# A decoder trunk's cross-attention weights, turned by 32x32 blocks and a DRAM round trip instead of by TensorE

## The chip, the cores and the metric

The kernel runs on one core of a Trainium2 chip. Its time is the device time of one execution in microseconds (us), the median of several runs. TensorE (PE in the profile) multiplies matrices, VectorE (DVE), ScalarE (ACT) and GpSimd (POOL) work on elements, and SyncE (SP) issues most of the DMA transfers; in this kernel POOL issues the stores. Each engine takes its instructions in the order in which they stand in its own queue.

## The reference

One inference step of a decoder trunk of width 1024, for a prompt of 1024 tokens and 8 sample tokens, in float32. A normalised input goes through one wide projection; its parts feed three branches (gated linear attention, causal pooling, cross attention into 256 memory tokens), which are projected, gated, summed, projected once more and added to the input. The change lies in the third branch, for the prompt:

```
def cross_attn(q, mk, mv):
    """q: (B,T,H,Dh); mk, mv: (B,M,H,Dh)."""
    s = jnp.einsum('bthd,bmhd->bhtm', q.astype(jnp.float32), mk.astype(jnp.float32)) * (XA_HEAD_DIM ** -0.5)
    p = jax.nn.softmax(s, axis=-1)
    o = jnp.einsum('bhtm,bmhd->bthd', p, mv.astype(jnp.float32))
```

There are 4 heads of dimension 256. The sample tokens have the same attention with cached keys and values of their own.

## The kernel before

**Products and streams.** The wide projection is cut into 40 pairs of output blocks, each computed by seven products of half-size operands; a product has two slots of 12 matmuls of 128x258. Every float32 matmul is done as three (`mm3`, lines 238 to 242) on a high part and a low remainder of each operand: hi*hi, hi*lo, lo*hi. So every operand is first split: ACT writes the high part (L221, or L224 with a scale), DVE the remainder (L222 or L225). The results in PSUM banks `px` (six) are evacuated by ACT (L550 and others) and DVE (L598, L615).

**What fills the gaps.** After each slot, `fill()` moves other work on: a generator of steps, each with a cost, is advanced until its share of the work is done. In the stage from about 120 to 370 us this work is cross attention. It puts its matmuls between slots of the projection, on two PSUM banks of their own (`pz`). PE's and SP's instructions stand in the order in which the program writes them; ACT's, DVE's and POOL's are ordered by a scheduler.

**Cross attention.** The prompt is handled in 16 chunks, 4 heads with 4 chunks of 256 tokens each. `cross_steps` (L811) runs step s as a pipeline: scores of chunk s; the split of the queries of s+1 and the load of those of s+2; at s % 4 == 2 the load of the next head's memory; part of the sample tokens' work; the value matmuls of chunk s-2; more sample work; the next head's memory at s % 4 == 3; the weights of chunk s-1; three more parts of sample work. A chunk's tokens lie as j (two halves of 128) times 128 rows. `cross_scores` gives p, 128 tokens by 2 x 256 memory tokens: maxima on DVE (L688), exponentials on ACT, division on DVE (L695). The value matmuls need it the other way, memory tokens on the partitions. `cross_weights` (L698) does this by four PE transposes of 128x128 into a `pz` bank (L703), from which `split_r` writes pTh (ACT, L221) and pTl (DVE, L222) into two new tiles. `cross_values` multiplies (L714), ACT copies the result out (L715), POOL stores it as `mixsc` (L716).

**Tiles.** Tiles of 128x512 come from a ring of 14 (`R`, `NR`), reused in turn: an allocation waits until the tile of 14 allocations earlier is no longer read. A chunk takes six: xq (the queries, whose remainder is written in place), xqsh, p, pTh, pTl and xo.

**Sample tokens.** `cross_sample` is interleaved with this: the query row is stored to DRAM by POOL (`xqs`, L731), loaded again for all partitions (`qb`, L746), multiplied with cached keys on DVE (`kc`, L756); after a softmax the cached values (`vc`, four loads at a time) meet PE at L796. All loads, the projection's raw weights (`raw`, L293) too, are issued by SP in one queue.

Of the kernel before, what the change touches and what calls it, by code (L numbers as in the profile page):

```python
# [18 lines left out]
P = 128  # L19
# [5 lines left out]
NH = 4  # L25
# [8 lines left out]
CT = 256  # L34
# [13 lines left out]
def trunk_kernel(ctx: ExitStack, tc: tile.TileContext,  # L48
# [3 lines left out]
    nc = tc.nc  # L52
# [21 lines left out]
    def act(out, x, func, **kw):  # L74
        i = nc.scalar.activation(out, x, func, **kw)
        if func in (AF.Sigmoid, AF.Silu):
            table["others"].append(i)
            for e in table["exps"]:
                tc.add_manual_dep(i.ins, e.ins.name, nosync, reason="table set")
        else:  # L80
            tc.add_manual_dep(i.ins, table["load"].ins.name, nosync, reason="table set")
            table["new"].append(i)
        return i
# [15 lines left out]
    def PZ():  # L99
        return ps.tile([P, 512], F32, tag="pz", name="pz", bufs=2)  # L100

    def shaped(t, shape):
        n = math.prod(shape)
        t = t[:, :n]
        if len(shape) == 2:
            t = t.rearrange("p (a b) -> p a b", a=shape[0])
        elif len(shape) == 3:
            t = t.rearrange("p (a b c) -> p a b c", a=shape[0], b=shape[1])
        return t
# [4 lines left out]
    def R(shape, dt=F32, name="r"):  # L114

        return shaped(wk.tile([P, 512], dt, tag="ring", name=name, bufs=NR), shape)
# [16 lines left out]
    def tiny(w, name="t", bufs=8):  # L133
        return wk.tile([P, 16], F32, tag="t", name=name, bufs=bufs)[:, :w]


    ident = cp.tile([P, P], F32, name="ident")
# [63 lines left out]
    def scratch(n, name, shape):  # L201
        return [dr.tile(list(shape), F32, name=f"{name}{i}") for i in range(n)]

    PAIR = (P, 4, HT)
    xq_scr, v_scr = scratch(NH, "xqs", (NS, 256)), scratch(NH, "vs", (NS, 256))
    acc_scr = [scratch(NK, f"acc{n}_", (P, TT)) for n in range(2)]
    mkv_scr = [scratch(NH, f"mkvs{o}", (P, 2, DV)) for o in range(2)]
    al_scr = scratch(2, "als", (P, HT))
# [9 lines left out]
    def split(dst_hi, dst_lo, src, scale=None):  # L218

        if scale is None:  # L220
            last["hi"] = nc.scalar.activation(dst_hi, src, AF.Copy)  # L221
            last["lo"] = nc.vector.tensor_tensor(dst_lo, src, dst_hi.bitcast(F32), op=ALU.subtract)  # L222
        else:
            nc.scalar.activation(dst_hi, src, AF.Copy, scale=scale)  # L224
            nc.vector.scalar_tensor_tensor(dst_lo, src, scale, dst_hi.bitcast(F32), op0=ALU.mult, op1=ALU.subtract)  # L225

    def split_r(src, shape, name, scale=None):
        hi, lo = R(shape, F32R, name + "h"), R(shape, F32R, name + "l")
        split(hi, lo, src, scale)
        return hi, lo  # L230

    def split_in(x, shape, name, scale=None):

        hi, lo = R(shape, F32R, name + "h"), x.bitcast(F32R)
        split(hi, lo, x, scale)
        return hi, lo

    def mm3(out, lh, ll, rh, rl, start, stop, more=False):

        nc.tensor.matmul(out, lhsT=lh, rhs=rh, start=start, stop=False, skip_group_check=more)  # L240
        nc.tensor.matmul(out, lhsT=lh, rhs=rl, start=False, stop=False, skip_group_check=more)  # L241
        nc.tensor.matmul(out, lhsT=ll, rhs=rh, start=False, stop=stop, skip_group_check=more)  # L242
# [401 lines left out]
    def mix_chunk(n, h, c):  # L644
        return mix_scr[n][h][:, :, c * CT:(c + 1) * CT]

    def loaded(src, shape, name, alloc=None):
        t = (alloc or R)(shape, name=name)
        nc.sync.dma_start(out=t, in_=src)
        return t  # L650
# [8 lines left out]
    cross = {}  # L659

    def cross_load(h):
        cross["raw", h] = [loaded(mkv_scr[o][h], [2, DV], "mkv") for o in range(2)]

    def cross_memory(h):
        mk, mv = cross["raw", h]
        t = PZ()
        for i in range(2):
            for a in range(2):
                nc.tensor.transpose(t[:, i * NM + a * P:i * NM + (a + 1) * P], mk[:, a, i * P:(i + 1) * P], ident)
        cross["mk", h] = split_r(t.rearrange("p (i m) -> p i m", i=2), [2, NM], "mkT")  # L670
        cross["mv", h] = split_in(mv, [2, DV], "mvs")
# [7 lines left out]
    def cross_scores(h, c):  # L679
        xh, xl = cross["q", h, c]  # L680
        mh, ml = cross["mk", h]
        t = PZ()
        for j in range(2):
            for i in range(2):
                cs = slice(j * P, (j + 1) * P)
                mm3(t[:, j * NM:(j + 1) * NM], xh[:, i, cs], xl[:, i, cs], mh[:, i], ml[:, i], i == 0, i == 1)
        nm = tiny(2, "nm")
        nc.vector.tensor_reduce(nm, t.rearrange("p (j m) -> p j m", j=2), axis=AX.X, op=ALU.max, negate=True)  # L688
        p = R([2, NM], name="p")
        sm = tiny(2, "sm")  # L690
        for j in range(2):
            act(p[:, j], t[:, j * NM:(j + 1) * NM], AF.Exp, bias=nm[:, j:j + 1], accum_out=sm[:, j:j + 1])
        nc.vector.reciprocal(sm, sm)
        for j in range(2):
            nc.vector.tensor_scalar(p[:, j], p[:, j], sm[:, j:j + 1], None, op0=ALU.mult)  # L695
        cross["p", h, c] = p

    def cross_weights(h, c):  # L698
        p = cross["p", h, c]
        t = PZ()  # L700
        for a in range(2):
            for j in range(2):
                nc.tensor.transpose(t[:, (2 * a + j) * P:(2 * a + j + 1) * P], p[:, j, a * P:(a + 1) * P], ident)  # L703
        cross["pT", h, c] = split_r(t.rearrange("p (a t) -> p a t", a=2), [2, CT], "pT")

    def cross_values(h, c):
        ph, pl_ = cross["pT", h, c]
        vh, vl = cross["mv", h]
        g = R([2, CT], name="xo")
        t = PZ()  # L710
        for i in range(2):
            cs = slice(i * P, (i + 1) * P)
            for a in range(2):
                mm3(t[:, i * CT:(i + 1) * CT], vh[:, a, cs], vl[:, a, cs], ph[:, a], pl_[:, a], a == 0, a == 1)  # L714
        nc.scalar.activation(g, t.rearrange("p (i t) -> p i t", i=2), AF.Copy)  # L715
        nc.gpsimd.dma_start(out=mix_chunk(2, h, c), in_=g)  # L716

# [93 lines left out]
    def cross_steps():  # L811
        def scores(n):
            cross_scores(n // 4, n % 4)

        def memory(n):
            if n % 4 == 0:
                cross_memory(n // 4)

        def weights(n):
            cross_weights(n // 4, n % 4)  # L820

        def values(n):
            cross_values(n // 4, n % 4)

        samples = chain_of(cross_sample(h) for h in range(NH))
        cross_load(0)
        cross_memory(0)
        cross_fetch(0, 0)
        yield 2
        cross_queries(0, 0)  # L830
        cross_fetch(0, 1)
        for s in range(16 + 2):
            if s < 16:
                scores(s)
                yield 3
                if s + 1 < 16:
                    cross_queries(*divmod(s + 1, 4))
                if s + 2 < 16:
                    cross_fetch(*divmod(s + 2, 4))
            if s % 4 == 2 and s < 14:  # L840
                cross_load(s // 4 + 1)
            if s >= 1:
                yield next(samples, 0)
            if 0 <= s - 2:
                values(s - 2)
                yield 1.7
            if s >= 1:
                yield next(samples, 0)
            if s % 4 == 3 and s < 15:
                memory(s + 1)  # L850
                yield 2
            if 0 <= s - 1 < 16:
                weights(s - 1)
                yield 1.7
            for _ in range(3):
                if s >= 1:
                    yield next(samples, 0)
        yield from samples

    def chain_of(gens):  # L860
        for g in gens:
            yield from g
# [423 lines left out]
    with tc.issue_after(last["hi"].ins), tc.issue_after(last["lo"].ins):  # L1286
        prepare(1)
        for j in (4, 6):
            r = squares(x_t[j:j + 2], 4 + j)
# [104 lines left out]
    for u, (o, n, d) in enumerate(units):  # L1394
# [11 lines left out]
        for t, (c0, cw) in zip(ts, CH):  # L1406
            cs = slice(c0, c0 + cw)
# [48 lines left out]
    for hf, order in enumerate(ORDERS):  # L1456
        for tb in order:
# [13 lines left out]
            if hf == 0:  # L1471
                x = (E([D], name="y") if tb < 8 else RAW("ys").rearrange("p a b -> p (a b)"))[:m]
                nc.sync.dma_start(out=x, in_=x_p[tb * P:(tb + 1) * P] if tb < 8 else x_s)
                rows_[tb], sums[tb] = x, wk.tile([P, 4], F32, tag="yq", name="yq", bufs=9)[:m]
            x, sq = rows_[tb], sums[tb]
# [5 lines left out]
            n, a = hf, 0  # L1481
            for b in ends:
                t = ts if tb == 8 else begun.pop(0) if begun else PX()
                cs = slice(512 * hf + a, 512 * hf + b)
# [12 lines left out]
                n, a = n + 1, b  # L1497
# [3 lines left out]
            if end:  # L1501
                r = rstd_of(sq[:, 2:3], 1.0 / D, more=so_far)
# [6 lines left out]
            r = rstd_of(sq[:, 0:1], 1.0 / D, m)  # L1509
# [34 lines left out]
```

## Time and profile before

| What | Number |
|---|---|
| Median of 3 runs | 1454.77 us (1454.15 to 1455.24) |
| Span of the profiled execution | 1455.4 us, 0.6 above the median |
| PE busy | 1430.4 us, 98% |
| DVE, ACT, POOL busy | 62%, 47%, 11% |
| DMA | 259.46 MB, mean 178 GB/s |

The profile is of one execution, and its span is that execution's own time. A row of a group gives the line, the engine, the operation, out<-in with the tiles' names, the shape and the count, then the busy time, the mean ns of one, and the idle time of the engine just before, with what ended it ("<-PE pz L703"). In a timeline a row is start, duration, engine, line. PEld is PE's weight load, which runs beside its matmuls; a matmul's duration is longer than the distance to the next, since matmuls overlap in the pipeline. SPq is SP's DMA queue. A landing is the time from the issue of a DMA until its data is there.

### The profile page before, as it was taken

The page shows a single profiled execution, that of the slowest core. Times are in us where ns is not written, and L with a number is a line of the kernel's source. Part 1 is how long each engine was busy: PE and PEld are TensorE (multiplying, and loading weights), DVE is VectorE, ACT ScalarE, POOL GpSimd, SP SyncE. Part 2 cuts the span into 40 slices and gives each one's busy share as a digit, 9 for nine tenths or more (in the row PEclk, how much of TensorE's full clock was granted, in tenths as well). Part 3 has the DMA queues.
Part 4 walks back from the last instruction along what each step waited for, and adds up shares of the span by engine and source line. Part 5 has one row for each costly group of instructions (what it writes and reads, how often), then busy time and mean ns, then how long its engine had stood idle before and what let it go on. Part 6 is the DMA issues. An engine that isn't in the chain of part 4 may idle for free.

```text
span 1455.4 us, 28240 instructions
## 1 busy us (share of the span) xinstructions
PE 1430.4 (98%) x10817; PEld 1369.2 (94%) x10817; DVE 896.6 (62%) x2075; ACT 688.4 (47%) x1591; POOL 159.0 (11%) x297
## 2 busy tenths in 40 slices
PE   7999999999999999999999999999999999999998
PEld 6899999999899999999999999999999999999876
DVE  6955756656576767766756668785672443544436
ACT  5744444444565666656554445454472333233312
POOL 3211111111011111111111111110010000000000
PEclk9999999999999999999999999999999999999999
DMA  9345675756445453553544455464595677632633
GB/s 322 127 165 183 204 226 173 227 174 201 158 146 178 149 176 121 166 175 118 180 139 141 153 187 187 147 197 155 191 304 159 219 252 249 231 120 67 230 119 116
DMA packets 181843, 259.46 MB, mean 178 GB/s; under 512 B 20540, under 2 KB 130900, under 8 KB 181700
## 3 DMA queue, kind: packets, MB, share of 16 engines
q1 hardware_dynamic: 159900, 183.87, 40.8%
q0 software_dynamic: 21664, 73.59, 13.3%
q8 instruction: 85, 1.39, 0.4%
q14 instruction: 50, 0.41, 0.1%
q10 hardware_dynamic: 144, 0.20, 0.0%
HBM read 180.47 MB, written 77.59 MB: 177 GB/s over the span
## 4 chain that ended last, share of the span: by engine, by line
PE 87%; DMA 6%; DVE 4%; ACT 1%; issue 1%; SPq 0%; DVEq 0%; POOL 0%; ACTq 0%
PE px L240 25%; PE px L241 24%; PE px L242 24%; PE pz L242 2%; PE pz L240 2%; PE pz L241 2%; DMA qb<-xqs 2%; DMA raw<-in_w_in_dram 1%; DMA vc<-in_cache_mem_v_dram 1%; DVE kc L756 1%; PE pz L942 1%; PE pz L924 1%; DMA wm<-in_w_mv_dram 1%; PE pz L796 1%; PE pz L926 1%
## 5 line engine op out<-in xcount | busy, mean ns | idle before, releaser
L242 PE MATMUL px<-bh,wbl 128*128 128x384 f32 (+1 forms) x576 | 184.1, 320 | 0.0
L241 PE MATMUL px<-bl,wbh 128*128 128x384 f32 (+1 forms) x576 | 184.1, 320 | 0.0
L240 PE MATMUL px<-bh,wbh 128*128 128x384 f32 (+1 forms) x576 | 183.8, 319 | 0.0
L550 ACT ACTIVATE r<-px 128x258 f32<-128x258 f32 x240 | 89.8, 376 | 46.7 <-PE px L242 46.1
L240 PEld LDWEIGHTS px<-bh,wbh 128*128 128x128 f32 x576 | 108.4, 188 | 0.0
L241 PEld LDWEIGHTS px<-bl,wbh 128*128 128x128 f32 x576 | 108.2, 188 | 0.0
L242 PEld LDWEIGHTS px<-bh,wbl 128*128 128x128 f32 x576 | 108.2, 188 | 0.0
L240 PE MATMUL px<-ot,s1h 128*128 128x258 f32 x320 | 93.9, 293 | 0.0
L240 PE MATMUL px<-ot,s3h 128*128 128x258 f32 x320 | 93.4, 292 | 0.0
L240 PE MATMUL px<-o,a12h 128*128 128x258 f32 x320 | 93.3, 291 | 0.0
L240 PE MATMUL px<-o,s4h 128*128 128x258 f32 x320 | 93.0, 291 | 0.2 <-DVE c L615 0.2
L240 PE MATMUL px<-o,a11h 128*128 128x258 f32 x320 | 92.9, 290 | 0.0
L240 PE MATMUL px<-ot,a22h 128*128 128x258 f32 x320 | 92.9, 290 | 0.0
L240 PE MATMUL px<-ot,s2h 128*128 128x258 f32 x320 | 92.3, 288 | 0.0
L241 PE MATMUL px<-o,a11h 128*128 128x258 f32 x320 | 91.0, 284 | 0.3 <-DVE o L222 0.3
L242 PE MATMUL px<-o,a12l 128*128 128x258 f32 x320 | 90.7, 283 | 0.0
L241 PE MATMUL px<-o,a12h 128*128 128x258 f32 x320 | 90.6, 283 | 0.0
L241 PE MATMUL px<-ot,s2h 128*128 128x258 f32 x320 | 90.1, 282 | 0.5 <-DVE ot L222 0.5
L242 PE MATMUL px<-o,a11l 128*128 128x258 f32 x320 | 90.6, 283 | 0.0
L241 PE MATMUL px<-ot,a22h 128*128 128x258 f32 x320 | 90.5, 283 | 0.0
L242 PE MATMUL px<-ot,s3l 128*128 128x258 f32 x320 | 90.4, 283 | 0.0
L241 PE MATMUL px<-ot,s3h 128*128 128x258 f32 x320 | 90.4, 282 | 0.0
(469 smaller groups left out, 4587.3 us busy)
## 6 DMA issues: line engine op xcount, KB each, us to landing
raw<-in_w_in_dram SPq DMA_DIRECT2D x80, 512.0 KB, 3.8
msc<-c POOLq DMA_DIRECT2D x24, 516.0 KB, 4.4
brsc<-c POOLq DMA_DIRECT2D x24, 516.0 KB, 4.0
sig<-msc SPq DMA_DIRECT2D x24, 516.0 KB, 6.0
mix<-mixsc SPq DMA_DIRECT2D x48, 256.0 KB, 4.5
brr<-brsc SPq DMA_DIRECT2D x48, 256.0 KB, 5.3
wbr<-in_w_branch_dram SPq DMA_DIRECT2D x24, 512.0 KB, 5.5
acc<-sig POOLq DMA_DIRECT2D x16, 516.0 KB, 6.1
```

The source lines that it names most:

```text
L240: nc.tensor.matmul(out, lhsT=lh, rhs=rh, start=start, stop=False, skip_group_check=more)
L241: nc.tensor.matmul(out, lhsT=lh, rhs=rl, start=False, stop=False, skip_group_check=more)
L242: nc.tensor.matmul(out, lhsT=ll, rhs=rh, start=False, stop=stop, skip_group_check=more)
L550: nc.scalar.activation(r, acc[c][:, :QT], AF.Copy)
L756: nc.vector.tensor_tensor_reduce(kc[:, a, :], kc[:, a, :], qb[:, bb, :], scale=1.0, scalar=0.0, op0=ALU.mult, op1=ALU.add, accum_out=sc[:, ...
L796: nc.tensor.matmul(t[32 * j:32 * j + 32, :DV], lhsT=pm[:, a, 4 * i + j, :], rhs=vc[j][:, a, :], start=a == 0, stop=a == 1)
L924: nc.tensor.matmul(t[0:64, 0:P], lhsT=ki[:, 0:64], rhs=qi, start=True, stop=True)
L926: nc.tensor.transpose(t[:, P:2 * P], kt, ident)
L942: nc.tensor.matmul(to, lhsT=kiqi[:, 1, cs], rhs=st, start=False, stop=True)
```

## The change

The PE transposes go. At the end of `cross_scores` DVE transposes p in blocks of 32x32 in one instruction (into pt), and POOL stores the result with four DMAs into a DRAM scratch `pts`, so that the blocks come to their places there, in 256 runs of 256 B each DMA. A new `cross_turned(h, c)` lets SP load the turned weights back as tile pT, 128 x 2 x 256, in runs of 1 KB. It is called in step s for chunk s-1, behind the query load of s+2 and ahead of the sample work. `cross_weights` then only splits pT: the high part into a new tile, the remainder in place. The tokens of a chunk come back in another order (q, j, c: four blocks, two halves, 32 tokens); `cross_values` reads them so that its result is in the old order, with the moving operand in runs of 32 values. A chunk takes seven ring tiles: xq, xqsh, p, pt, pT, pTh, xo.

```diff
+    pt_scr = scratch(4 * NH, "pts", (8, 32, 4, 64))
...
             nc.vector.tensor_scalar(p[:, j], p[:, j], sm[:, j:j + 1], None, op0=ALU.mult)
-        cross["p", h, c] = p
+        pt = R([512], name="pt")
+        nc.vector.transpose(pt.rearrange("p (b j c) -> p j b c", j=2, c=32), p.rearrange("p j (b c) -> p j b c", c=32))
+        for q in range(4):
+            nc.gpsimd.dma_start(out=pt_scr[4 * h + c][:, :, q, :].rearrange("b r x -> r b x"),
+                                in_=pt[32 * q:32 * q + 32].rearrange("r (b x) -> r b x", b=8))
 
     def cross_weights(h, c):
-        p = cross["p", h, c]
-        t = PZ()
-        for a in range(2):
-            for j in range(2):
-                nc.tensor.transpose(t[:, (2 * a + j) * P:(2 * a + j + 1) * P], p[:, j, a * P:(a + 1) * P], ident)
-        cross["pT", h, c] = split_r(t.rearrange("p (a t) -> p a t", a=2), [2, CT], "pT")
+        cross["pT", h, c] = split_in(cross["pr", h, c], [2, CT], "pT")
+
+    def cross_turned(h, c):
+        cross["pr", h, c] = loaded(pt_scr[4 * h + c].rearrange("(a b) r q x -> (b r) a (q x)", a=2), [2, CT], "pT")
 
     def cross_values(h, c):
...
-                mm3(t[:, i * CT:(i + 1) * CT], vh[:, a, cs], vl[:, a, cs], ph[:, a], pl_[:, a], a == 0, a == 1)
+                rh, rl = (x[:, a].rearrange("p (q j c) -> p j q c", q=4, j=2) for x in (ph, pl_))
+                mm3(t[:, i * CT:(i + 1) * CT].rearrange("p (j q c) -> p j q c", j=2, q=4), vh[:, a, cs], vl[:, a, cs],
+                    rh, rl, a == 0, a == 1)
...
             if s % 4 == 2 and s < 14:
                 cross_load(s // 4 + 1)
+            if 0 <= s - 1 < 16:
+                cross_turned(*divmod(s - 1, 4))
             if s >= 1:
                 yield next(samples, 0)
```

On POOL the four stores of each chunk stand ahead of the store of an earlier chunk's result; the eight of the first two chunks stand ahead of the store of the sample's query row (`xqs`). On DVE the block transpose stands, at most chunks, right between the division that completes p and the remainder split of the next chunk's queries.

SP's queue at the loads of the first cached values, before:

```order
L649 DMA xq<-xqsc_171 128x2x256
L293 DMA raw<-in_w_in_dram 128x4x256
L649 DMA xq<-xqsc_171 128x2x256
L649 DMA vc<-in_cache_mem_v_dram 128x2x256 x4
L293 DMA raw<-in_w_in_dram 128x4x256
```

And after:

```order
L650 DMA xq<-xqsc_187 128x2x256
L650 DMA pT<-pts_134 128x2x256
L294 DMA raw<-in_w_in_dram 128x4x256
L650 DMA xq<-xqsc_187 128x2x256
L650 DMA pT<-pts_135 128x2x256
L650 DMA vc<-in_cache_mem_v_dram 128x2x256 x4
L294 DMA raw<-in_w_in_dram 128x4x256
```

The reload of chunk s-1 stands behind the query load of chunk s+2, ahead of the raw weights and the cached values.

ACT's queue around the first chunk's high split, before (a, s are weights of the projection, r copies out of px, qn the sample's query row):

```order
L730 ACTIVATE qn<-pz 8x256
L221 ACTIVATE pTh<-pz 128x512
L221 ACTIVATE a22h<-raw 128x512
L550 ACTIVATE r_1705<-px 128x258
L75 ACTIVATE p,sm<-pz,nm 128x256 x2
```

And after:

```order
L735 ACTIVATE qn<-pz 8x256
L222 ACTIVATE a22h<-raw 128x512
L551 ACTIVATE r_1729<-px 128x258
L222 ACTIVATE pTh<-pT 128x512
L222 ACTIVATE a12h<-raw 128x512
L75 ACTIVATE p,sm<-pz,nm 128x256 x2
```

The high split has moved behind the weight split a22h and one copy, and stands ahead of the weight split a12h and the exponentials of chunk 2.

## The prediction

> **What bounds the kernel now.** I read the page first: busy time and the chain that ended last.
>
> ```profile
> PE 1430.4 (98%) x10817; PEld 1369.2 (94%) x10817; DVE 896.6 (62%) x2075; ACT 688.4 (47%) x1591; POOL 159.0 (11%) x297
> PE 87%; DMA 6%; DVE 4%; ACT 1%; issue 1%; SPq 0%; DVEq 0%; POOL 0%; ACTq 0%
> ```
>
> TensorE (PE) is busy for 98% of the span and carries 87% of the chain. Next came the table of windows, since a share of the span is an average over stages. Its columns are the window, its length, then busy us and instructions of PE, PE's weight loads, VectorE (DVE), ScalarE (ACT) and GpSimd (POOL), the granted clock, the DMA engines' share and GB/s.
>
> ```profile
> 120.00:370.00 250.00, 243.49 (x2053) 236.02 (x2052) 155.07 (x403) 110.95 (x267) 28.22 (x53) 0.99 0.61 192
> 370.00:700.00 330.00, 328.02 (x2694) 312.67 (x2693) 228.00 (x601) 203.45 (x554) 41.89 (x70) 1.00 0.47 154
> 700.00:1100.00 400.00, 398.81 (x3292) 395.12 (x3291) 274.83 (x605) 203.89 (x450) 47.69 (x78) 1.00 0.56 182
> ```
>
> The first row is the cross-attention stage, where all of the change lies. PE is idle there for 6.5 of 250 us, and in the two stages behind for 2.0 of 330 and 1.2 of 400: what the stage gives back, the rest carries to the end almost whole. DVE is busy 62% of the stage, ACT 44%, POOL 11%. Third, the list of PE's waits between 120 and 375 us (total, times, longest):
>
> ```profile
> PE pz L796 <- DMA vc<-in_cache_mem_v_dram: 1.9, 2, 1.5
> PE pz L782 <- DVE ps L777: 1.5, 1, 1.5
> PE pz L240 <- ACT xqsh L224: 1.4, 1, 1.4
> PE pz L242 <- DVE xq L225: 1.3, 2, 1.0
> PE pz L240 <- DVE pTl L222: 1.2, 1, 1.2
> PE pz L770 <- DVE mkTl L222: 0.7, 1, 0.7
> ```
>
> Eight waits, 8.0 us, none of them of the transposes for their input and none of a projection for a weight. So in this stage PE's own issue time is the limit, and an instruction taken from PE is worth what it took of that.
>
> **What is removed.** One chunk's four transposes in PE's timeline (start, duration), the same tile in the group over all 16 chunks, and a second chunk:
>
> ```profile
> 182.28 0.28 PE L242 MATMUL px<-ot,a22l 128*128 128x258 f32 x1
> 182.40 0.60 PE L703 MATMUL pz<-ident,p 128*128 128x128 f32 x4
> 182.96 0.28 PE L241 MATMUL px<-o,a12h 128*128 128x258 f32 x1
> L703 PE MATMUL pz<-ident,p x64: 270/272/275, 137.3 to 357.5; 128*128 128x128 f32 x64
> 198.20 0.28 PE L242 MATMUL px<-ot,s3l 128*128 128x258 f32 x1
> 198.88 0.28 PE L241 MATMUL px<-ot,s3h 128*128 128x258 f32 x1
> ```
>
> The matmul ahead of the group starts at 182.28, the second one behind it at 182.96. Without the group two ordinary steps lie between; such a step is 0.12 us (182.28 to 182.40). The group costs 0.68 - 0.24 = 0.44 us, and the second chunk the same (198.20 to 198.88). Times 16 that is **7.0 us**. The four lines' own busy time, 0.60 x 16 = 9.6 us, counts overlap with the pipeline and is the upper bound.
>
> Also removed is one use of the two PSUM banks (pz) per chunk. At one place PE waited 1.2 us because the low split, pTl, still read such a bank (the last row but one of the waits): now the split reads SBUF, and the wait can go. That is **1.2 us**, or 0 if the bank is held by something else.
>
> **What is added on ACT and DVE.** The splits stay, one hi and one lo per chunk, with another source. Groups of the stage, last numbers busy us and mean ns:
>
> ```profile
> L688 DVE TENSOR_REDUCE nm<-pz 128x2 f32<-128x512 f32 x16 | 11.0, 688 | 9.8 <-PE pz L242 9.8
> L222 DVE TENSOR_TENSOR pTl<-pz,pTh 128x512 fp32r<-128x512 f32 x16 | 11.0, 687 | 5.7 <-ACT pTh L221 5.1 <-DMA mixsc<-xo 0.5
> L225 DVE SCALAR_TENSOR_TENSOR xq<-xq,xqsh 128x512 fp32r<-128x512 f32 x16 | 11.0, 685 | 0.0
> L224 ACT ACTIVATE xqsh<-xq 128x512 fp32r<-128x512 f32 x16 | 10.1, 631 | 0.0
> L221 ACT ACTIVATE pTh<-pz 128x512 fp32r<-128x512 f32 x16 | 9.5, 595 | 5.9 <-PE pz L703 5.4 <-DMA mixsc<-xo 0.2
> L240 PE MATMUL pz<-pTh,mvsh 128*128 128x256 f32 x64 | 18.1, 283 | 0.0
> ```
>
> From SBUF the hi split takes 631 instead of 595 ns, 0.6 us in all, and the lo split 685 instead of 687: nothing on an ACT that is idle over half of the stage. The new 32x32 transpose is not in the trace. All DVE rows over 128x512 elements lie at 0.69 us, whatever they do; I take that, 16 x 0.69 = 11 us, which lifts DVE from 155 to 166 of 250. Were it twice as slow, DVE would be at 71%. It stands ahead of the next chunk's query split in DVE's order, and the scores wait for that split at one place near the start of the stage:
>
> ```profile
> 131.52 0.39 PE L242 MATMUL pz<-mkTh,xq 128*128 128x256 f32 x1 [0.98 <-DVE xq L225]
> ```
>
> There 0.98 becomes 0.98 + 0.69: **+0.7 us**. The only other wait for xq, 0.3 us of the 1.3 listed, is of the first scores, ahead of any p.
>
> **The round trip.** Rows for its parts: a POOL issue, the landings (KB each, median us), the last from the start of the program, whose 64 KB go in short runs.
>
> ```profile
> 148.93 0.69 POOL L716 DMA_DIRECT2D mixsc<-xo  x1 [1.87 <-ACT xo L715]
> mixsc<-xo POOLq DMA_DIRECT2D x15, 256.0 KB, 3.9
> xq<-xqsc SPq DMA_DIRECT2D x14, 256.0 KB, 5.1
> xqs<-qn POOLq DMA_DIRECT2D x4, 8.0 KB, 1.6
> wa<-in_w_in_dram POOLq DMA_DIRECT2D x1, 64.0 KB, 7.4
> ```
>
> Each chunk issues 4 stores of 64 KB on POOL, 256 runs each like mixsc<-xo: 4 x 0.69 = 2.8 us, 44 us in the stage on an engine busy 28 of 250. Such a store lands in 1.6 to 7.4 us; I take 3.9, the row of equally many runs. The reload has the size and the runs of xq: 5.1 us behind an issue of 0.53. From p to pT that makes 0.69 + 2.8 + 3.9 + 0.5 + 5.1 = **13.0 us**, 10.7 to 16.5 by the bounds. What there is of time, at the first chunk and at a late one whose reload stands behind xq in SP's queue:
>
> ```profile
> 129.92 0.61 DVE L695 TENSOR_SCALAR p<-p,sm 128x256 f32<-128x256 f32 x2
> 140.84 0.39 ACT L550 ACTIVATE r<-px 128x258 f32<-128x258 f32 x1 [0.93 <-PE px L242]
> 146.41 0.28 PE L240 MATMUL pz<-pTh,mvsh 128*128 128x256 f32 x1
> 283.83 0.53 SPq L649 DMA_DIRECT2D xq<-xqsc  x1
> 289.95 0.60 ACT L221 ACTIVATE pTh<-pz 128x512 fp32r<-128x512 f32 x1 [1.03 <-PE pz L703]
> 300.24 0.28 PE L240 MATMUL pz<-pTh,mvsh 128*128 128x256 f32 x1
> ```
>
> First chunk: p is done at 130.5, pT lands at 143.5. In the new order ACT comes to the hi split behind the r copy, at 141.2, and would stand for 2.3 us, with a weight split and the exponentials of the next chunk but one queued behind it; DVE's lo split likewise, with a row maximum behind. The value matmuls want pT at 146.4, and hi and lo splits of 1.3 us end at 144.8: late for ACT, in time for PE. Late chunk: xq is issued at 283.83, the reload right behind at 284.4, pT is there at 289.5 to 290.0, and ACT split pT at 289.95 in any case. From 300.24 on PE needs it, 10 us later. So the trip is hidden but for short stands of ACT and DVE, which PE sees only if a PSUM evacuation behind them is late.
>
> What is queued behind the reload on SP: key, value, query and weight loads of the stage. Where p's trip is not over, they wait too. At the first chunk SP stood for the sample's query row anyway (issued at 137.25 by POOL, now behind eight stores). The next tight place is this:
>
> ```profile
> 175.62 2.31 SPq L649 DMA_DIRECT2D vc<-in_cache_mem_v_dram  x4
> 184.39 0.42 PE L796 MATMUL pz<-vc,pm 128*32 128x256 f32 x4
> vc<-in_cache_mem_v_dram SPq DMA_DIRECT2D x32, 256.0 KB, 4.1
> ```
>
> Four loads issued by 177.9 are used at 184.39; with a landing of 4.1 us some 2.4 us are spare. The reload, now ahead of them, takes 0.5 of it, and more if its ring tile is free late. I set the new waits of this kind, and those of ACT and DVE, at **1.5 us** in all, between 0 and 4 (two late places at 2 us each).
>
> **The memory system.** All packets of the stage's two large queues:
>
> ```profile
> q1 hardware_dynamic: 33008, 34.80, 47.0%
> q0 software_dynamic: 3776, 12.95, 13.3%
> ```
>
> 47.0% of 16 engines over 250 us is 1880 us, 57 ns for a packet of 1.05 KB. The reloads are 4096 of those: 233 us, 5.8% of the engines. The stores are 16,384 runs of 256 B, between 14 ns (by bytes) and 57 ns: 5.7% to 23%. The DMA share goes from 0.61 to 0.72 to 0.90. The Trainium skill, page "DMA: Bandwidth & Descriptors", section "Specifications", says that transfers below 512 B make the DMA engine read, modify and write. By it the upper end is the likelier, and the time is that of the late trip below. No row here has runs of 256 B by themselves. I keep the loads' times as they are and leave the upper end to a rival.
>
> **Sum.** -7.0 - 1.2 + 0.7 + 1.5 = -6.0 us on the profiled span of 1455.4, or 1449.4. The median of the runs is 1454.77, 0.6 below that span, so the time told is **1448.8**. About 0.2%, 2.9 us, is what a measurement here tells from no change (the three runs differ by 1.1).
>
> **Rivals.**
>
> *Strided weights on PE (slower).* The 192 value matmuls (three groups of 64 as the row of pTh,mvsh) now read their moving operand in runs of 32 values, 128 B, in permuted order. No matmul of the trace reads so. If such a matmul no longer streams at one step, it goes from 0.12 towards its own 0.283 us: at most +31 us, at half rate +23. From +31 ns each it eats the 6.0; I take half rate, -6.0 + 23.0 = **1471.8**. For it: the order is new to PE. Against: within each run nothing changes. The Trainium skill, "Advanced Engine Details and Errata", section "Memory Cachelines", says SBUF works in 16-byte lines, and two hits on a line hide the latency; it calls non-contiguous access slow for matmuls only under PSUM. The PSUM output stays in order here, so by that page the cost would be none. Chance 0.06.
>
> *The trip is late at every chunk (slower).* With the DMA engines at 0.9, or POOL's issues slower beside a busier DVE, the 13.0 us and the splits' 1.3 pass the 15.9 that the first chunk has from p (130.5) to the values (146.4). Then ACT and DVE stand at every chunk with evacuations behind them, and loads stand behind the reload on SP. It eats the gain when PE loses 0.37 us per chunk (6.0 / 16). At twice that, 0.75 us, it is 1448.8 + 12 = **1460.8**. For it: a DMA share of 0.61 already, and the first chunk's reserve of 1.6 us (144.8 to 146.4), which the upper bound of 16.5 us passes. Against: 10 us of reserve at the late chunk. Chance 0.08. A milder form, at a few chunks alone, eats 3 to 6 us: **1453.3** with 4.5, no difference to be told. Chance 0.16.
>
> *Nothing is gained,* because the pipeline hides the transposes and PE takes the same time without them: 1454.8. Against it the 0.44 us, twice to the hundredth. Chance 0.02.
>
> *More is gained:* the 9.6 of the transposes, the 1.2, and no new wait: 1454.77 - 10.8 = **1444.0**. For it: banks pz come free earlier at every chunk. Chance 0.08.
>
> **Numbers.** The forecast has 0.60. With the larger gain, faster has 0.68; the milder late trip and nothing gained make 0.18 for no change; late trips at every chunk and strided weights make 0.14 for slower. The range goes from 1445, just above the larger gain, to 1458, which holds the 4 us bound of the new waits and the milder late trip. It leaves out the strided weights (0.06), most of the late trips (0.07) and half of the larger gain (0.04).
>
> **What would show it.** Right: no PE rows of the transposes, value matmuls still 0.12 us apart, PE's idle time in the stage within 3 us of 6.5, end of stage some 6 us earlier. Wrong: value matmuls further apart, or PE waits on ACT's or DVE's weight splits, on px evacuations, or on vc and raw loads of more than 3 us in sum.

## The result, and the profile after

The changed kernel takes 1463.15 us (four runs, 1460.83 to 1465.33), the kernel before 1454.46 us beside it. The ratio is 1.0057, 95% interval 1.0044 to 1.0071: **slower by 0.57%, 8.3 us**, where 6.0 us less was forecast, and outside the range given. The profiled execution was a mild one, 2.3 below the median, with a span of 1459.1 us, only 3.7 above the profile of before. (A span is in nearly all runs 1.7 us shorter than the time told; by that the profile of before is of an execution of some 1457 us, above its median.) The runs without a profile cannot be taken apart, so what follows explains 3.7 us row by row and the rest by the comparisons of times.

The page after, busy time and the chain that ended last:

```profile
PE 1427.9 (98%) x10753; PEld 1362.6 (93%) x10753; DVE 905.2 (62%) x2091; ACT 687.0 (47%) x1591; POOL 196.1 (13%) x361
PE 89%; DMA 4%; DVE 4%; issue 1%; ACT 1%; SPq 1%; POOL 0%; DVEq 0%; ACTq 0%
```

The 64 transposes are gone (10817 to 10753 matmuls), and PE is still 98% busy. The windows show where it was lost:

```profile
120.00:370.00 250.00, 235.32 (x1924) 223.79 (x1923) 161.68 (x415) 107.16 (x263) 65.55 (x117) 0.99 0.71 223
370.00:700.00 330.00, 329.86 (x2717) 314.44 (x2716) 226.80 (x597) 201.76 (x548) 41.34 (x69) 1.00 0.48 154
```

In the cross-attention stage PE is now idle for 14.7 us, against 6.5; the next stage has no loss. PE's waits between 120 and 380 us:

```profile
PE pz L801 <- DMA vc<-in_cache_mem_v_dram: 5.4, 3, 4.5
PE pz L775 <- DVE sc L761: 4.0, 3, 2.3
PE pz L241 <- ACT xqsh L225: 2.6, 2, 1.4
PE pz L243 <- DVE xq L226: 1.0, 2, 0.8
PE pz L787 <- DVE ps L782: 1.0, 1, 1.0
PE pz L241 <- ACT p L75: 0.6, 1, 0.6
```

Together 14.6 us, against 8.0. Of these, 10.4 us are waits not for anything of the prompt's 16 chunks, but for the **sample tokens' own attention**: the cached values (vc), the scores that DVE sums up (sc) and the weights of the softmax (ps). Before, these three had 3.4 (vc 1.9, ps 1.5, sc none). All other waits are 4.2 us, against 4.6. The waits for turned weights, which the change concerns, are not in the list at all.

The same two projection matmuls in both timelines, at the stage's two ends, before:

```profile
119.65 0.28 PE L241 MATMUL px<-ot,a22h 128*128 128x258 f32 x1
381.12 0.28 PE L241 MATMUL px<-o,s4h 128*128 128x258 f32 x1
```

and after:

```profile
118.21 0.28 PE L242 MATMUL px<-ot,a22h 128*128 128x258 f32 x1
384.81 0.28 PE L242 MATMUL px<-o,s4h 128*128 128x258 f32 x1
```

The stage took 261.5 us and takes 266.6: +5.1 with 7.0 us of transposes taken out, so some 12 us came in. 6.6 are the waits, net. The rest hides in what counts as busy. The sample tokens' value products (128 matmuls in both), before and after:

```profile
L796 PE MATMUL pz<-vc,pm 128*32 128x256 f32 x128 | 9.9, 386 | 1.9 <-DMA vc<-in_cache_mem_v_dram 1.9
```

```profile
L801 PE MATMUL pz<-vc,pm 128*32 128x256 f32 x128 | 14.4, 413 | 5.5 <-DMA vc<-in_cache_mem_v_dram 5.4
```

4.5 us more busy time with the same work. It comes in eight rows of 16: the first, second, third and fifth took 1.07, 1.22, 1.07 and 1.07 us before and take 2.08, 1.88, 3.83 and 3.18, with slow clock or a late part of the values inside them; only the last two are shorter than before. The worst place, SP's queue, before:

```profile
235.66 0.53 SPq L649 DMA_DIRECT2D xq<-xqsc  x1
236.89 11.13 SPq L649 DMA_DIRECT2D vc<-in_cache_mem_v_dram  x8
```

SP's queue after, with the DVE and PE rows that belong to it:

```profile
237.81 0.53 SPq L650 DMA_DIRECT2D xq<-xqsc  x1
242.59 0.37 SPq L650 DMA_DIRECT2D pT<-pts  x1
243.52 12.43 SPq L650 DMA_DIRECT2D vc<-in_cache_mem_v_dram  x7
...
241.81 0.71 DVE L698 STREAM_TRANSPOSE pt<-p 128x512 f32<-128x512 f32 x1
...
251.27 3.83 PE L801 MATMUL pz<-vc,pm 128*32 128x256 f32 x16 [4.48 <-DMA vc<-in_cache_mem_v_dram]
```

The reload of one chunk is not issued behind xq at 238.3, but at 242.6, in the moment in which DVE's block transpose ends (241.81 + 0.71). With stores of the chunk long landed, it waits for its **ring tile**. This is the eighth reload, and the transpose is the ninth: it belongs to the next chunk, whose p is taken only four allocations ahead of the reload's tile. So the tiles are not handed out strictly in turn, as "Tiles" above has it: what the wait fits is that the reload got the tile which that p had just left. The values' loads behind it are issued 6.6 us later than before (2.2 of it because xq itself is later), and PE stands for them for 4.48 us. Over the stage SP's list of waits has two rows that the trip brings:

```profile
SPq L650 <- DMA pts<-pt: 12.3, 4, 7.4
SPq L650 <- DVE pt L698: 9.8, 3, 4.1
```

The first is the trip itself, not yet over (7.8 us at the first reload) or holding a tile that a load of xq needs (4.5 us); the second is three reloads that wait for the next chunk's transpose. Back at that place, PE is then slow as well, as the granted clock (third number from the end) shows in two windows behind the wait:

```profile
252.00:255.40 3.40, 3.40 (x15) 1.29 (x15) 0.00 (x0) 0.27 (x1) 0.00 (x0) 0.50 0.09 30
256.00:259.40 3.40, 3.40 (x31) 3.40 (x30) 1.38 (x2) 0.91 (x2) 0.00 (x0) 1.00 0.84 272
```

Half the clock for 3.4 us: a long wait costs 1.7 us on top of itself. (The 15 matmuls against 31 show more than the clock, since most of them are the late value products.) The stage has two such stretches, both behind a wait of the sample chain (the other from 170 us on, behind a wait for sc). Before, it had one, at 124.5 us, behind a wait of the prompt's first scores for xqsh.

### The profile page after: what moved, and what is told of

It is laid out like the page before. It is cut to its first block, busy times and chain, and to the rows that moved or that the text cites. A ratio compares the mean times of both kernels' runs of the same rounds, so it can differ in the third digit from the quotient of the medians.

```text
span 1459.1 us, 28334 instructions
## 1 busy us (share of the span) xinstructions
PE 1427.9 (98%) x10753; PEld 1362.6 (93%) x10753; DVE 905.2 (62%) x2091; ACT 687.0 (47%) x1591; POOL 196.1 (13%) x361
## 4 chain that ended last, share of the span: by engine, by line
PE 89%; DMA 4%; DVE 4%; issue 1%; ACT 1%; SPq 1%; POOL 0%; DVEq 0%; ACTq 0%
PE px L241 25%; PE px L242 25%; PE px L243 25%; PE pz L243 2%; PE pz L242 2%; PE pz L241 2%; DMA qb<-xqs 2%; DMA vc<-in_cache_mem_v_dram 2%; PE pz L949 1%; PE pz L801 1%; PE pz L931 1%; DMA x<-in_x_prompt_dram 1%; DVE kc L761 1%; PE pz L933 1%; PE pz L893 0%
## 5 line engine op out<-in xcount | busy, mean ns | idle before, releaser
L241 PE MATMUL px<-ot,s3h 128*128 128x258 f32 x320 | 93.3, 291 | 0.0
L243 PE MATMUL px<-ot,s1l 128*128 128x258 f32 x320 | 90.4, 283 | 0.0
```

## The experiments

Five theories, as they were set up and fell. **A**: the reload stands in SP's one queue, and the sample tokens' loads behind it come late. **B**: a chunk takes seven ring tiles instead of six, so loads wait for a tile. **C**: the trip's packets slow other transfers. **D**: DVE's added transposes make the work behind them late. **E**, formed after the first eight runs: the sample tokens' chain stands in PE's fixed order without any reserve, so whatever touches it is paid, by A to D alike. (In the profile of before PE already waits for vc and ps, 3.4 us, so at these reads there is none.) Every kernel was timed beside the kernel before, and a ratio to it is given with its interval; "0.31%" below is of some 1454 to 1455 us. One caution holds for all: ACT's, DVE's and POOL's orders are made anew for each kernel, so an effect of 0.2 to 0.3% may partly be that order. In this section PE's waits are those between 120 and 380 us.

**The trip left out.** The stores, the reload and the DVE transpose are gone, and unturned weights go to the value matmuls:

```
-        pt = R([512], name="pt")
-        nc.vector.transpose(...)
...
+        cross["pr", h, c] = p
```

> The changed kernel without the trip: no transpose on DVE, no stores, no reload; p itself is split and goes to the value matmuls unturned (so the attention's result is another), still read in strided runs, six ring tiles a chunk. All theories: the saving alone, 16 x 0.44 = 7.0 us and perhaps 1.2 of the bank wait, 1446 to 1449 us, stores and waits for vc and sc as before. If the strided reading by the value matmuls cost something, it would be seen here: at half rate 1470.

1451.02 us, 0.9979 (0.9968 to 0.9989): 3.1 us gained, not 6 to 8. So even with no trip at all less than half of the saving arrives. In its profile the stage has nearly the same PE idle time as before, but three stretches at half clock instead of one; before, and without the trip:

```profile
120.00:380.00 260.00, 252.01 (x2124) 243.27 (x2123) 157.61 (x411) 114.43 (x276) 29.81 (x56) 0.99 0.62 195
```

```profile
120.00:380.00 260.00, 251.62 (x2094) 242.20 (x2093) 162.45 (x426) 115.74 (x285) 30.21 (x57) 0.98 0.62 195
304.20:307.60 3.40, 3.40 (x22) 2.98 (x15) 0.37 (x1) 0.39 (x1) 0.00 (x0) 0.50 0.51 160
```

The last row is one of the two extra stretches. Both stand behind reads of the sample tokens: a wait of 3.1 us ahead of the value products (L797), for which the profile names no releaser, and one of 2.3 us for ps. So with nothing added, PE waits 5.7 us at the sample tokens' reads, against 3.4: part of what is taken from PE comes back as waits, as it would if PE only arrived earlier at reads whose data come no sooner.

**The reload on POOL's queue.**

```
-        cross["pr", h, c] = loaded(pt_scr[...]..., [2, CT], "pT")
+        cross["pr", h, c] = R([2, CT], name="pT")
+        nc.gpsimd.dma_start(out=cross["pr", h, c], in_=pt_scr[...]...)
```

> The changed kernel with one edit: the reload of the turned weights is issued by POOL, behind that chunk's four stores, and no longer by SP. Theory A (the reload stands in SP's one queue, and the sample tokens' key, query and value loads behind it come late): PE's waits for sc and vc fall from 9.4 us to about the 2 of before, no clock drop beyond the one of before, 1447 to 1451 us. Theory B (seven ring tiles a chunk instead of six: loads wait for a free tile): the same tiles are taken, so SP still waits for them, 1457 to 1463. Theory C (the trip's packets slow all landings): as many packets, 1458 to 1463.

1460.82 us, 1.0045 (1.0030 to 1.0059), against 1.0057 of the change. Theory A alone is not it: the intervals overlap. PE's waits for vc and sc did fall, from 9.4 to 3.0 us, nearly as A had it, but one for ps rose to 5.1, and all waits together are 15.3 us, against 14.6.

**Transpose and stores added to the kernel before.**

```
         cross["p", h, c] = p
+        pt = R([512], name="pt")
+        nc.vector.transpose(...)
+        for q in range(4):
+            nc.gpsimd.dma_start(out=pt_scr[...], in_=pt[32 * q:32 * q + 32]...)
```

> The kernel before, its PE transposes kept, with the block transpose on DVE and the four stores per chunk added and their result unused; no reload. Seven ring tiles a chunk. Theory A: nothing stands in SP's queue, so only the 0.7 us of the first query split: 1454 to 1457. Theory B: loads wait for tiles as in the changed kernel, 1459 to 1465. Theory C: two thirds of the trip's added DMA time are the stores', landings of vc and qb grow from 4.0 and 4.1 towards 4.8 and 5.3: 1459 to 1465.

1473.73 us, 1.0138 (1.0122 to 1.0154). 19 us, with no reload at all, so a loss of this size needs no A. It isn't quite the change's loss, though: besides 5.6 us for vc, PE here waits 5.8 us for pTl, the split of the PE transposes' result, which the changed kernel doesn't have.

**A larger ring.**

```
-NE = 30
-NR = 14
+NE = 29
+NR = 16
```

> The changed kernel with a ring of 16 tiles instead of 14, the room taken from one of the 30 tiles of the projection's operands. Theory A: SP's reload still waits for the stores, little changes, 1457 to 1463. Theory B: SP no longer waits for tiles (its waits for DVE pt, 9.8 us, and for PE pz, 21 us, shrink by half or more) and the loss goes: 1447 to 1452. Theory C: 1458 to 1463.

1509.98 us, 1.0390 (1.0367 to 1.0413). A miss: the missing operand tile costs by itself, all along the program (between 700 and 1100 us, where no cross attention is left, PE is idle for 10.3 us, against 1.2), and nothing about the ring follows.

**A seventh ring tile and nothing else,** in the kernel before:

```
+        nc.vector.memset(R([512], name="pt")[:, :8], 0.0)
```

> The kernel before with nothing but a seventh ring tile per chunk: it is taken where the changed kernel takes pt, and DVE writes 8 columns of it, used by nobody. No transpose, no stores, no reload. Theory B (ring: loads at the head of SP's queue wait for a tile that matmuls of the same step still read, and the cached keys and values behind them come late): most of the loss of the added stores' kernel, 1462 to 1475 us, with SP's waits for PE pz up from 20.6 us. Theory C (packets) and theory D (the DVE transpose): no change, 1453 to 1456.

1458.99 us, 1.0031 (1.0017 to 1.0044). The time agrees with theory B, at a smaller size than expected. The list of SP's waits has a row that the kernel before has not, with the dummy's own name:

```profile
SPq L649 <- DVE pt L697: 18.4, 5, 9.8
```

PE does not wait longer in this profile, 7.8 us against 8.0, which is of one of the kernel's fastest executions (1456.5 us). So how the tile costs the time is not shown, and part of 0.31% may be the order.

**Transpose and stores with pt in a tile of its own,** in the kernel before:

```
-        pt = R([512], name="pt")
+        pt = w2
```

> The kernel before with the block transpose and the four stores per chunk added and unused, as in the added stores' kernel, but pt in a tile of its own (the place of the gate weights w2, which are then loaded at the end of the stage), so six ring tiles a chunk. Theory B: 1454 to 1458, against 1473.7 with pt in the ring. Theories C and D: still 1468 to 1475.

1462.92 us, 1.0051 (1.0036 to 1.0066). Against the same work with pt in the ring, 1.0138, the tile is worth over 12 us here, more than the dummy. In the ring it is held until its stores have landed; that this makes the difference is not shown, since in the ring version's profile only 0.6 us of waits are listed as for these stores. And 0.51%, 7.4 us, remain without it.

**The changed kernel with pt in a tile of its own** (the same edit):

> The changed kernel with pt in a tile of its own (the place of w2, loaded at the end of the stage): six ring tiles a chunk as before the change, the trip itself unchanged. Theory B: the loss goes, 1447 to 1452 us, PE's waits in the stage 8 us or less. Theory A (the reload stands in SP's queue): little changes, 1457 to 1462, since SP still waits for the stores. Theory C: 1457 to 1462.

1457.36 us, 1.0018 (1.0007 to 1.0029). About two thirds of the loss against the kernel before are gone, but it isn't faster. At the place shown above SP now issues as the kernel before did:

```profile
235.52 0.47 SPq L648 DMA_DIRECT2D pT<-pts  x1
...
236.82 12.94 SPq L648 DMA_DIRECT2D vc<-in_cache_mem_v_dram  x8
```

The reload follows xq at once, and the values' loads stand at 236.82, before at 236.89. At this place B is shown: the tile delayed the queue. But PE's waits did not fall to 8 us or less, as B had it: they are 14.0 us, against 14.6 with pt in the ring, of them 8.0 for vc, ps and sc. They stand at other reads now.

**The same with the reload on POOL.**

> The same with the reload issued by POOL as well, so that nothing of the trip stands in SP's queue and six ring tiles are taken. Theory B alone: as with SP's reload, 1447 to 1452. Theories A and B both at work: better than that kernel by 2 us or more, 1446 to 1449. Theory C: 1457 to 1462 still.

1463.55 us, 1.0059 (1.0044 to 1.0073): worse than with SP's reload. Why was not settled; the two differ in POOL's, DVE's and ACT's orders too. PE waits 10.9 us for ps, sc and vc. So in every version of the changed kernel up to here that computes the whole, the sample tokens' reads cost PE 8 to 11 us of waits, at changing places.

**Without the sample tokens' attention:** its loads, products, softmax and stores are left out of the kernel before, and of the changed kernel, with the spacing of the steps kept:

```
-        samples = chain_of(cross_sample(h) for h in range(NH))
+        costs = [0.5] * 2 + [1.2, 1] * 3 + [1] + [0.5] + [1.2, 0.5] * 2 + [1.2, 0.5, 0.5] * 2 + [1.2]
+        samples = iter([1.2, 0.5, 0.5] + costs * NH)
```

> The kernel before without the sample tokens' cross attention: none of its loads, DVE, ACT, PE or POOL work, its result left at zero; the order and the spacing of all else as they were. It serves as the base for the changed kernel treated alike. Theory E (the sample tokens' chain of query row, products on DVE, softmax, cached values stands in PE's fixed order without reserve, and what the trip adds makes it late): PE's waits in the stage go to 3 us or less, 1438 to 1446 us by the matmuls left out and the waits. Theory C (packets slow the loads of the weights and queries): the same here, since this is the base.

> The changed kernel, seven ring tiles and SP's reload, without the sample tokens' cross attention, as the kernel before was cut. Theory E: what the trip delays is gone, so the saving shows whole: 6 to 8 us below the kernel before cut in the same way. Theories B and C (tiles or packets make the prompt's own loads late): at or above that kernel, -1 to +8 us.

1432.13 us (0.9858, 0.9843 to 0.9873) and 1426.17 us (0.9816, 0.9803 to 0.9829), four runs each. **Here the change gains 6.0 us**, with seven ring tiles, SP's reload and the trip's packets all in place. The same two matmuls at the stage's ends, the kernel before without samples:

```profile
125.11 0.38 PE L240 MATMUL px<-o,a12h 128*128 128x258 f32 x1
380.07 0.28 PE L241 MATMUL px<-o,s4h 128*128 128x258 f32 x1
```

and the changed kernel without them:

```profile
124.16 0.28 PE L241 MATMUL px<-o,a12h 128*128 128x258 f32 x1
371.90 0.28 PE L242 MATMUL px<-o,s4h 128*128 128x258 f32 x1
```

254.96 against 247.74 us: 7.2 less. PE's waits within these bounds are 0.9 us in the one,

```profile
PE pz L242 <- DVE xq L225: 0.9, 1, 0.9
```

and 2.0 in the other:

```profile
PE pz L241 <- ACT xqsh L225: 1.2, 1, 1.2
PE pz L243 <- DVE xq L226: 0.8, 1, 0.8
```

The first has one stretch at half clock, at its start, and the second none:

```profile
125.10:128.50 3.40, 3.40 (x18) 3.40 (x17) 1.24 (x4) 1.54 (x5) 0.00 (x0) 0.50 0.33 131
```

7.2 is thus 1.7 of clock, less 1.1 of waits, and 6.6 for the transposes. (The first profile is of the slowest of its four runs, 1436.1 us.) This is the run that decides: the saving is there, and the prompt's own path hides the trip. What eats it is the sample tokens' chain, at whose reads PE stands in the traces above. That these reads are late because they have no reserve in PE's order is argued: without the chain the stage's load is smaller as well, with the DMA engines busy 52% between 120 and 380 us instead of 71%. The load does not make the prompt's own reads late: at all other reads PE waits 4.2 us in the changed kernel, 4.6 in the one before.

**The parts alone, in the kernel before.** The transpose alone, into its own tile:

```
+        pt = w2
+        nc.vector.transpose(pt..., p...)
```

> The kernel before with only the block transpose on DVE added, 16 x 0.7 us, into a tile of its own and unused; no stores, six ring tiles. Of the 7.8 us that transpose and stores cost together with pt in its own tile: theory D (DVE, in order, comes later to the sample chain and the query splits) puts most here, 1459 to 1463; theory C almost none, 1455 to 1457.

1458.12 us, 1.0033 (1.0023 to 1.0044). The stores alone, of p in its ring tile:

```
+        pt = p.rearrange("p j m -> p (j m)")
+        for q in range(4):
+            nc.gpsimd.dma_start(out=pt_scr[...], in_=pt[32 * q:32 * q + 32]...)
```

> The kernel before with only the four stores per chunk added, of p itself as it stands and unused; no block transpose, six ring tiles (p's is held until it is stored). Theory C (256-byte runs slow the other transfers): most of the 7.8 us, 1460 to 1464. Theory D: almost nothing, 1455 to 1457.

1467.24 us, 1.0095 (1.0079 to 1.0110). That is more than transpose and stores cost together from an own tile (1.0051), so most of it would be p's tile, held until the stores have landed; the profile has only 0.9 us of waits for these stores. Stores of an own tile, in which DVE writes 8 columns:

```
+        pt = w2
+        nc.vector.tensor_copy(pt[:, :8], p[:, 1, :8])
+        for q in range(4):
+            nc.gpsimd.dma_start(out=pt_scr[...], in_=pt[32 * q:32 * q + 32]...)
```

> The kernel before with the four stores per chunk added, of a tile of its own of which DVE writes 8 columns after p (so that the stores are issued where the trip issues them); no transpose, six ring tiles, no tile held. The stores' packets and POOL's issues alone. Theory C: 1457 to 1460. If packets cost nothing and the loss of the stores' kernel came from p's held tile: 1454 to 1456.

1457.97 us, 1.0021 (1.0011 to 1.0030). So packets and POOL's issues cost some 3 us, the transposes some 5, in the kernel before. These prices can't be carried over to the change: in these runs, as in the two with transpose and stores above, PE waits 1.8 to 6.3 us for pTl (1.2 in the kernel before), and the changed kernel has no such wait.

**An empty step more ahead of each of the chain's PE reads,** in the own-tile version, the kernel before and the changed one, with the amount of work that `fill()` spreads over the stage (`WORK_A`) raised from 493 to 501:

```
         yield 0.5
+        yield 0.5
```

> The changed kernel with pt in its own tile and one empty step more in the sample tokens' chain ahead of each of its four kinds of PE reads (scores, softmax, first and second cached values), so that a stretch of the projection lies between; nothing else moved. Theory E (no reserve in the chain): PE's waits in the stage fall from 12.6 to 5 us or less, 1446 to 1451 us. If instead the chain's or the trip's throughput (DMA share, DVE) is the limit, the waits only move: 1455 to 1459.

> The kernel before with the same four empty steps per head. Theory E: it had some 4 us of the chain's waits and their clock drops, so 1450 to 1454 us; the own-tile version with the steps is 3 to 6 us below it. Otherwise no change, 1454 to 1457.

> The changed kernel, pt in the ring, with the same empty steps. Theory E: 1448 to 1454 us, above the own-tile version by the ring's part that is left. Throughput: 1459 to 1464.

1468.70 (1.0099, 1.0083 to 1.0115), 1466.80 (1.0081, 1.0064 to 1.0098) and 1467.26 us (1.0087, 1.0070 to 1.0103): all slower. The steps pushed the last head's chain behind the chunks, where little work lies between its links: in the kernel before its scores were read at 357 us, ahead of the last chunk's values at 369, and with the steps at 370, behind these values at 353. The kernel before with the steps then waits like this:

```profile
PE pz L771 <- DVE sc L756: 7.7, 1, 7.7
```

With them the three kernels come out within 2 us of each other: none shows the saving. They don't tell how much reserve would do.

**The sample tokens' loads on POOL's queue,** in the kernel before and the own-tile version, with `nc.gpsimd` given as queue for kc, vc and qb:

```
-        nc.sync.dma_start(out=t, in_=src)
+        (queue or nc.sync).dma_start(out=t, in_=src)
```

> The kernel before with the sample tokens' loads (kc, qb, vc) issued by POOL instead of SP. If the chain is late because its loads stand in SP's queue behind others that wait: PE's 4 to 5 us of waits for sc, ps and vc and their clock drops go, 1448 to 1453 us. If it is late by DVE's and ACT's order or by its own length: 1453 to 1457; slower than that if POOL's stores of results and projections now stand behind loads that wait for a tile.

> The changed kernel with pt in its own tile, and kc, qb and vc issued by POOL, so that SP has the reload, the queries and the weights alone. If SP's queue is the place: 1446 to 1451, below both kernels. If POOL's queue becomes a new one, in which the trip's stores stand behind loads that wait for a tile: 1458 or more.

1472.22 (1.0120, 1.0099 to 1.0141) and 1465.57 us (1.0076, 1.0055 to 1.0098). POOL became the queue in which others stand: in the kernel before it waits for the tiles of these loads,

```profile
POOL kc L649 <- DVE sc L756: 44.1, 11, 6.1
POOL vc L649 <- PE pz L796: 21.6, 4, 9.3
```

and the stores behind them come late. No kernel that computes all of the reference beat the kernel before.

## Why the prediction was wrong

- **The transposes' 7.0 us**: near. 6.6 in the stage, once the sample chain is out; the time is then 6.0 less. But the step "an instruction taken from PE is worth what it took of that" did not hold with the chain in: even without the trip only 3.1 us arrived. The sign stood in the list of waits: where PE already waits (vc, ps: 3.4 us), arriving earlier gains nothing.
- **The value matmuls' strided operand at no cost**: right. The groups of the changed kernel, with 283 ns before:

```profile
L242 PE MATMUL pz<-pT,mvsh 128*128 128x256 f32 x64 | 18.0, 281 | 0.0
L698 DVE STREAM_TRANSPOSE pt<-p 128x512 f32<-128x512 f32 x16 | 11.3, 706 | 0.2
L222 ACT ACTIVATE pTh<-pT 128x512 fp32r<-128x512 f32 x16 | 10.0, 626 | 17.3 <-DMA pT<-pts 16.4 <-DMA pts<-pt 1.0
```

- **DVE's transpose at 0.69 us, the hi split at 0.63**: right as durations (0.706, 0.626). As a cost it was put at 0.7 us, at the second scores. There it was near: they waited 0.98 us before and wait 1.93 now, first for the high split of the queries, then for the remainder.

```profile
128.56 0.38 PE L241 MATMUL pz<-mkTh,xqsh 128*128 128x256 f32 x1 [1.17 <-ACT xqsh L225]
129.82 0.39 PE L243 MATMUL pz<-mkTh,xq 128*128 128x256 f32 x1 [0.76 <-DVE xq L226]
```

As the only cost of a busier DVE it was too little: the transpose alone, in the kernel before, costs 0.33%, 4.8 us.
- **The round trip of 13.0 us and the memory system**: near. The stage after:

```profile
q1 hardware_dynamic: 36608, 38.27, 51.3%
q0 software_dynamic: 5824, 17.15, 19.5%
...
vc<-in_cache_mem_v_dram SPq DMA_DIRECT2D x28, 256.0 KB, 5.3
pts<-pt POOLq DMA_DIRECT2D x64, 64.0 KB, 4.4
pT<-pts SPq DMA_DIRECT2D x16, 256.0 KB, 4.1
```

Stores 4.4 us (3.9 taken), reload 4.1 (5.1 taken). The stores came as 2048 packets more on q0 with 4.2 MB, 2 KB each, not as 16,384 of 256 B, and took 6.2% of the engines, at the low end of 5.7 to 23%. The Trainium skill, "DMA: Bandwidth & Descriptors", "Specifications", states that transfers below 512 B are read, modified and written; the DMA's share shows no such extra work here. But vc now lands in 5.3 instead of 4.1 us, and I had kept the loads' times as they were.
- **ACT and DVE stand for the trip, PE doesn't**: right. ACT stood 16.4 us for pT in six places, and PE has no wait on pT.
- **The bank wait of 1.2 us**: gone, as forecast.
- **The new waits**: here it failed, at the step "I set the new waits of this kind, and those of ACT and DVE, at **1.5 us** in all, between 0 and 4 (two late places at 2 us each)". By the two profiles the term came to some 12 us: the stage grew by 5.1 although 7.0 and 1.2 went out of it and only 0.9 came in at the second scores. PE's waits at the sample tokens' reads grew from 3.4 to 10.4 us, and these products' stretched rows and a drop of the clock added to them. Two things were wrong in it. I had followed the path of the chunk, from p to the values, and of the sample tokens one single load of vc; the rest of their chain (qb, the products on DVE, the scores, the second half of the values) passes the same SP queue and DVE as the trip at every chunk, and PE reads it at fixed places, at some of which it had to wait even before. And I wrote "more if its ring tile is free late" without counting: at the place shown the reload stood for its tile for over 4 us. By the times of the dummy and the own tile, a seventh tile a chunk comes with 4 to 6 us, of which part may be the scheduler's order. How much of the chain's lateness is its place in PE's order, and how much the load, stays open.
- **The rival "late at every chunk"** had the sign and nearly the size (1460.8), but another mechanism: not the chunk's own reserve ran out, and not PSUM evacuations behind ACT's waits, but four reads a head of another stream.

From no trip (0.9979) to the trip with its own tile (1.0018) is 0.39%, from there to the change (1.0057) again 0.39%, 5.7 us each: transposes, packets and reload the one, the seventh ring tile the other. This is by the times; the waits in the profiles of the last two are nearly equal (14.0 and 14.6 us). Within each half the order that the scheduler makes was not separated from the work itself.

## What to carry to other kernels

An engine that is 98% busy is worth relieving only as far as the streams that feed it stay ahead: list what each of its in-order reads waits on, the streams that the change does not touch too, and ask for their reserve. Before adding a tile to a shared ring, ask which instruction frees the tile that each load will take, and look at what stands behind the load that will wait for it. To test whether a saving is real, take out the stream that PE waits for, in both kernels: if the saving then appears, the rest is a question of lateness, not of work.

## What the runs showed of the hardware

A wait of PE costs more than its length. Behind waits of a few us the granted clock is 0.50 for 3.4 us: behind 4.48 us in the changed kernel (the two windows above), and behind only 1.91 us in the own-tile version, with 16 matmuls of the projection in 3.3 us instead of 30:

```profile
246.93 1.05 PE L799 MATMUL pz<-vc,pm 128*32 128x256 f32 x10 [1.91 <-DMA vc<-in_cache_mem_v_dram]
```

```profile
247.90:251.20 3.30, 3.30 (x16) 3.29 (x16) 0.00 (x0) 0.91 (x2) 0.00 (x0) 0.50 0.66 205
252.00:255.30 3.30, 3.30 (x30) 3.30 (x29) 1.42 (x3) 0.57 (x3) 0.00 (x0) 1.00 0.16 53
```

In the kernel before, a wait of 1.39 us of the first scores, followed by one of 0.29, stands ahead of such a stretch (16 matmuls at a granted clock of 0.51 between 124.5 and 127.9 us):

```profile
123.68 0.38 PE L240 MATMUL pz<-mkTh,xqsh 128*128 128x256 f32 x1 [1.39 <-ACT xqsh L224]
```

The length of the wait alone does not decide it: the changed kernel has the same wait of 1.39 us at the same place, and from there to 170 us its clock is full.

The Trainium skill, "TensorE: Matmul & The Clock Gate", Part 1, has the half rate set in after at least one idle window of about 3.4 us, and end after one busy window of that length. The length of the slow stretch agrees; the waits ahead of it were shorter here, 1.91 and 1.39 us.
